# Two more matrix products as block pairs of seven products, with the gates computed first

## Chip, core and metric

The kernel runs on one core of one Trainium2 chip. The metric is the time of one execution in microseconds of the device. TensorE (PE, with its weight loads PEld) multiplies, VectorE (DVE) and ScalarE (ACT) do the elementwise work, GpSimd (POOL) does next to nothing, and SyncE (SP) issues nearly all the transfers.

## The reference

A trunk of two layers on 512 tokens of width 1024, everything in float32. What matters here, for each layer:

```python
h = rmsnorm(x, g_mix)
z = h @ w_in          # q, k, v | ret q, k, v, g | gate_a | gate_b
A = sliding_window_sink_attention(...)          # 512 x 512
r = retention(...) * rsqrt(mean(r * r)) * silu(rg)   # 512 x 1024
mixed = sigmoid(gate_a) * (A @ w_a) + sigmoid(gate_b) * (r @ w_b)
x = x + mixed @ w_out
h2 = rmsnorm(x, g_mlp)
x = x + square(relu(h2 @ w_up)) @ w_down        # width 4096
```

`w_b` and `w_out` are 1024 x 1024. After the second layer comes a final rmsnorm.

## The kernel before

**Layout.** All activations lie transposed: 128 features on the partitions, 512 tokens along the free dimension, eight such tiles for a width of 1024. Each float32 operand is split into `hi` (rounded for the fast matmul format) and `lo` (the rest), and a product is three matmuls, hi x hi, hi x lo and lo x hi (lines 280 to 282, in `products`). ScalarE makes `hi` by a copy and VectorE `lo` by a subtraction, for activations in `split` and for weights in `split_until` (lines 235 and 236).

**Weights.** They come in units of 128 x 1024, in an order written out in `unit_order`. When a unit is taken (`unit`), the units up to three further on are split, and the loads run three ahead of the splits. There are three buffers each for raw units, `hi` and `lo`. So the fourth unit on can be split only when TensorE has finished this one.

**Products.** `chunk` makes one output tile from one unit (24 matmuls of 512 columns), `group` four output tiles from four units, with four PSUM banks at a time. `pair` makes two output tiles of the up product as a block product: the inputs are halved along the features and the tokens halved as well (`H` = 256), and seven products of such blocks, with sums and differences of blocks as operands, replace eight. Its weights come as four parts. `load_part` loads two units, and `add_part` forms the sums of the weights on VectorE (lines 207 to 215). The sums of the moving operand are made once a layer by `sum_input`, called from hooks inside the first up group, and split into `sums`. The seven products gather in three banks `a`, `e` and `b`; ScalarE copies `a` to `b` midway (line 1037), and VectorE finishes the two tiles.

**Order in a layer.** First come attention and retention, partly in the background between products. Then four `gate_b` tiles (lines 911 to 925), the rest of retention (`drain`), a group of four `w_b` tiles, the other four `gate_b` tiles by `chunk`, and four `w_b` tiles by `chunk`. `put_mixed` (lines 930 to 938) multiplies each `w_b` tile with its gate, adds the gated attention part, which stands in `x`'s buffer, and splits the sum into slots of its own. Then `x` is loaded again, four `w_out` tiles are made by a group and four by chunks, and `put_x` (lines 956 to 961) adds each to `x`, makes the scaled and split input `xh`, `xl` of the up product from it, and adds its square to the sum for the norm. The `w_up` group follows, and `rstd` of the norm is finished in its hooks (`first_hooks`). After it come two up pairs, and then down products and up pairs in turn (`mlp_sequence`). Tile's planner orders the instructions of each engine by a timeline of its own.

Of the kernel before, what the change touches and what calls it, by code (L numbers as in the profile page):

```python
# [17 lines left out]
P = 128  # L18
# [30 lines left out]
DELAY = 2  # L49


def unit_order():

    order = [("w_in", i) for i in range(4 + 2 + 8 + 2 + 4 + 2)]
    order += [("w_in", i) for i in range(22, 26)]
    order += [("w_a", i) for i in range(4)]
    order += [("w_in", i) for i in range(26, 42)]
    order += [("w_b", i) for i in range(4)]
    order += [("w_in", i) for i in range(42, 46)]
    order += [("w_b", i) for i in range(4, 8)]  # L60
    order += [("w_out", i) for i in range(8)]
    for what, q, i in mlp_sequence():
        if what == "first":
            order += [("w_up", u) for u in range(4)]
        elif what == "pair":
            order += [("pair", 8 * q + 2 * i, part) for part in range(4)]
# [48 lines left out]
def decoder(ctx, tc, xT, x_first, w_in, w_a, w_b, w_out, w_up, w_down, tables, decay, band, out):  # L115
# [17 lines left out]
    def big(name, dtype=F32):  # L133
        return tmp.tile([P, 2, T], dtype, tag="big", name=name, bufs=6)
# [57 lines left out]
    def load_part(i):  # L192
        layer, _, j, part = order[i]
        if part == 0:
            raws[i] = raw_tile()
            nc.sync.dma_start(raws[i][:, LEFT], w_up[layer, j][:, LEFT])
            raws[i + 3] = raw_tile()
            nc.sync.dma_start(raws[i + 3], w_up[layer, j + 1])
        elif part == 1:
            raws[i] = big("raw2").rearrange("p a t -> p (a t)")  # L200
            nc.sync.dma_start(raws[i][:, RIGHT], w_up[layer, j][:, RIGHT])

    def add_part(i):
        part = order[i][3]
# [12 lines left out]
    def split_until(n):  # L217
        while state["split"] < min(n, len(order)):
# [12 lines left out]
            for at in (LEFT,) if paired and order[i][3] == 3 else halves(i):  # L231
# [94 lines left out]
    def group(name, layer, moving, evacuates, meanwhile=None):  # L326
# [3 lines left out]
        for u in range(4):  # L330
            hi, lo = unit(name, layer)
            for j in range(2):
                k = 2 * u + j
                for c, ps in enumerate(banks):
                    cols = slice(j * T + c * P, j * T + (c + 1) * P)
                    products(ps, [((hi[:, cols], lo[:, cols]), moving[k])], k == 0, k == KD - 1)
# [5 lines left out]
    def two_chunks(name, layer, moving, evacuates):  # L342
# [9 lines left out]
        for ps, evacuate in zip(banks, evacuates):  # L352
            evacuate(ps)

# [125 lines left out]
    def layer_body(layer):  # L480
# [276 lines left out]
        rg, rg_next = {}, {}  # L757

        def put_rg(i):
            def put(ps):  # L760
                if i % 2 == 0:
                    two = big("z")
# [14 lines left out]
        ret = {}  # L777
# [7 lines left out]
        class Head:  # L785
# [53 lines left out]
            def finish(self):  # L839
                h = self.h  # L840
                for e in range(2):
# [5 lines left out]
                    ret[2 * h + e] = (hi, lo)  # L847
# [69 lines left out]
        def gate_tile(c):  # L917
            if c % 2 == 0:
                two = big("gb")
                gates.extend(two[:, j, :] for j in range(2))  # L920
# [9 lines left out]
        def put_mixed(c):  # L930
            def put(ps):
                m = temp("m")
                nc.vector.tensor_tensor(m, ps, gates[c], ALU.mult)
                nc.vector.tensor_tensor(m, m, mixed[c], ALU.add)
                hi, lo = slots.one(), slots.one()
                split(view(hi), view(lo), m)
                ms[c] = (hi, lo)

            return put

        rT = [tuple(view(s) for s in ret[k]) for k in range(KD)]
        group("w_b", layer, rT, [put_mixed(c) for c in range(4)])
        for c in range(4, KD):
            gate_tile(c)
            chunk("w_in", layer, xs, gate(gates[c]))
        for c in range(4, KD):
            chunk("w_b", layer, rT, put_mixed(c))
        for k in range(KD):
            slots.give(*ret.pop(k))
# [13 lines left out]

        mT = [tuple(view(s) for s in ms[k]) for k in range(KD)]
        group("w_out", layer, mT, [put_x(c) for c in range(4)])
        for c in range(4, KD):
            chunk("w_out", layer, mT, put_x(c))
        for k in range(KD):
            slots.give(*ms.pop(k))
# [5 lines left out]
        H = T // 2  # L975
        sums = [slots.four() for _ in range(4)]
        by_form = [t[0].rearrange("p a (b t) -> p (a b) t", t=H) for t in sums]

        def sum_input(ks):
# [6 lines left out]
            (b11, b12), (b21, b22) = ((t[:, :, :H], t[:, :, H:]) for t in b)  # L986
            f = [big("sums").rearrange("p a (b t) -> p (a b) t", t=H) for _ in range(2)]
            t1, t2, t3, t4 = f[0][:, 0:2, :], f[0][:, 2:4, :], f[1][:, 0:2, :], f[1][:, 2:4, :]
            hi, lo = by_form[ks // 2], by_form[2 + ks // 2]
            nc.vector.tensor_tensor(t1, b12, b11, ALU.subtract)  # L990
            nc.vector.tensor_tensor(t2, b22, t1, ALU.subtract)
            split(hi[:, 0:4, :], lo[:, 0:4, :], f[0])
            nc.vector.tensor_tensor(t3, b22, b12, ALU.subtract)
            nc.vector.tensor_tensor(t4, b21, t2, ALU.subtract)
            split(hi[:, 4:8, :], lo[:, 4:8, :], f[1])

        def form(j):
            return [tuple(by_form[2 * i + k // 2][:, 2 * j + k % 2, :] for i in range(2)) for k in range(4)]

        def block(half, tokens):  # L1000
            at = slice(tokens * H, tokens * H + H)
            return [(xh[:, k, at], xl[:, k, at]) for k in range(4 * half, 4 * half + 4)]
# [20 lines left out]
        def pair(q):  # L1023
            def multiply(ps, weights, left, moving, start=True):
                hi, lo = weights
                cols = [slice((0 if left else 4 * P) + k * P, (0 if left else 4 * P) + (k + 1) * P) for k in range(4)]
                products(ps, [((hi[:, c], lo[:, c]), m) for c, m in zip(cols, moving)], start, True, not start)

            a, e, b = (bank(ps_mm, "mm")[:, :H] for _ in range(3))
            eu, z = temp("eu"), big("z")
            part = unit("pair", layer)
            multiply(a, part, True, block(0, 0))
            nc.scalar.activation(b, a, AF.Copy)  # L1037
            multiply(e, part, False, form(0))
            nc.scalar.activation(eu[:, :H], e, AF.Copy)
            part = unit("pair", layer)  # L1040
            multiply(b, part, True, form(1), False)
            nc.scalar.activation(eu[:, H:], b, AF.Copy)
            multiply(a, part, False, block(1, 0), False)
            nc.vector.scalar_tensor_tensor(z[:, 0, :H], a, 0.0, rms_mlp.value[:, :H], ALU.max, ALU.mult)  # L1044
            part = unit("pair", layer)
            multiply(b, part, True, form(2), False)
            nc.vector.tensor_tensor(z[:, 1, H:], b, eu[:, :H], ALU.add)
            multiply(e, part, False, block(1, 1), False)
            nc.vector.tensor_tensor(z[:, 0, H:], e, eu[:, H:], ALU.add)
            part = unit("pair", layer)  # L1050
            multiply(b, part, True, form(3), False)
            later = rms_mlp.value[:, H:].unsqueeze(1).broadcast_to([P, 2, H])
            nc.vector.scalar_tensor_tensor(z[:, :, H:], z[:, :, H:], 0.0, later, ALU.max, ALU.mult)
            nc.vector.scalar_tensor_tensor(z[:, 1, :H], b, 0.0, rms_mlp.value[:, :H], ALU.max, ALU.mult)
            hi, lo, own = up_home()
            for i in range(2):
                nc.scalar.activation(z[:, i, :], z[:, i, :], AF.Square)
                split(hi[:, i, :], lo[:, i, :], z[:, i, :])
                up[q].append((hi[:, i, :], lo[:, i, :]))
            up_slots[q].extend(own)  # L1060
# [18 lines left out]
        for what, q, i in mlp_sequence():  # L1079
            if what == "first":  # L1080
                group("w_up", layer, xs, [put_up] * 4, first_hooks())
            elif what == "pair":
                pair(q)
                if (q, i) == (3, 3):
                    for t in sums:
                        slots.give(*t[1])
# [79 lines left out]

def _up_units(w):

    units = _units_group(w, np.arange(T))
    for i, u in enumerate(_units_chunks(w, np.arange(T, D_FF))):  # L1170
        units.append(np.concatenate([u[:, UNIT // 2 :], u[:, : UNIT // 2]], 1) if i % 2 else u)
    return units
# [41 lines left out]
def _laid_out(x, g_mix, w_in, sinks, w_a, w_b, w_out, g_mlp, w_up, w_down, g_final):  # L1214
# [13 lines left out]
        "w_b": _stack(w_b, _half_grouped),  # L1228
        "w_out": _stack(w_out, _half_grouped),
# [24 lines left out]
```

## Time and profile before

| | |
|---|---|
| median of 3 runs | 1512.94 us (1510.96 to 1513.03) |
| profiled execution, first to last instruction | 1511.4 us |
| granted TensorE clock, mean | 0.998 |
| transfers | 155.10 MB, mean 103 GB/s |

The profiled execution has no other time than its span; the median of the runs is 1.5 us above it. A busy PE in the page is modelled from overlapping matmuls, so the cost of one is read from the steps between starts. Idle time of an engine counts only where TensorE waits for it.

### The profile page before, as it was taken

How to read it: one execution, taken by the hardware profiler on the slowest of the kernel's cores; microseconds unless marked ns; L12 is line 12 of the kernel's file. 1: busy time of each engine (PE TensorE's matmuls, PEld its weight loads, DVE VectorE, ACT ScalarE, POOL GpSimd, SP SyncE). 2: the span in 40 equal slices, each digit the busy share in tenths (PEclk: the TensorE clock that was granted, in tenths of full speed). 3: DMA queues.
4: the chain of work that ended last, by engine and by line, in shares of the span. 5: the costliest groups of instructions: out<-in, count | busy, mean ns of one | idle time of the engine just before them, and what ended most of it. 6: DMA issues, size and time to landing. Idle time of an engine off the chain costs nothing.

```text
span 1511.4 us, 20498 instructions
## 1 busy us (share of the span) xinstructions
PE 1499.2 (99%) x8080; PEld 1302.2 (86%) x8080; DVE 1026.7 (68%) x1598; ACT 740.1 (49%) x1163; POOL 2.9 (0%) x13
## 2 busy tenths in 40 slices
PE   9999999999999999999999999999999999999997
PEld 7888888888888999989888888888888999889997
DVE  6877668754787666676678765777449866666664
ACT  6656455632564444444455742555327544444452
POOL 0000000000000000000000000000000000000000
PEclk9999999999999999999999999999999999999999
DMA  6422322233223232233442222222342232232331
GB/s 217 123 97 75 98 79 91 70 125 126 98 78 104 98 112 97 93 104 115 165 131 93 84 84 98 82 79 84 126 125 98 85 104 92 99 111 98 103 108 56
DMA packets 52640, 155.10 MB, mean 103 GB/s; under 512 B 6208, under 2 KB 8384, under 8 KB 52544
## 3 DMA queue, kind: packets, MB, share of 16 engines
q1 hardware_dynamic: 52400, 153.54, 30.6%
q8 instruction: 63, 1.03, 0.3%
q14 instruction: 33, 0.27, 0.1%
q10 hardware_dynamic: 144, 0.26, 0.0%
HBM read 146.96 MB, written 4.19 MB: 100 GB/s over the span
## 4 chain that ended last, share of the span: by engine, by line
PE 98%; ACT 1%; DVE 0%; DMA 0%; issue 0%; DVEq 0%
PE mm L280 29%; PE mm L281 29%; PE mm L282 29%; PE rv L280 2%; PE rv L281 2%; PE rv L282 2%; PE score L651 1%; PE pT L616 1%; PE r L281 1%; PE r L282 1%; PE r L280 1%; PE pv L637 0%; PE pv L636 0%; PE ssq L374 0%; PE ret L281 0%; PE ret L282 0%
## 5 line engine op out<-in xcount | busy, mean ns | idle before, releaser
L235 ACT ACTIVATE hi<-raw 128x1024 fp32r<-128x1024 f32 (+1 forms) x313 | 314.6, 1013 | 517.9 <-PE mm L281 430.6
L236 DVE TENSOR_TENSOR lo<-raw,hi 128x1024 fp32r<-128x1024 f32 (+1 forms) x314 | 362.6, 1164 | 162.0 <-ACT hi L235 161.1
L281 PE MATMUL mm<-r,hi 128*128 128x512 f32 (+1 forms) x1136 | 392.5, 346 | 0.0
L280 PE MATMUL mm<-r,hi 128*128 128x512 f32 (+1 forms) x1136 | 389.5, 346 | 1.0 <-ACT mm L1037 1.0
L282 PE MATMUL mm<-r,lo 128*128 128x512 f32 (+1 forms) x1136 | 388.5, 346 | 0.0
L280 PE MATMUL mm<-xh,hi 128*128 128x512 f32 (+1 forms) x1008 | 358.2, 357 | 0.9 <-ACT xh L290 0.9
L281 PE MATMUL mm<-xl,hi 128*128 128x512 f32 (+1 forms) x1008 | 356.8, 356 | 0.0
L282 PE MATMUL mm<-xh,lo 128*128 128x512 f32 (+1 forms) x1008 | 355.4, 356 | 0.0
L280 PEld LDWEIGHTS mm<-r,hi 128*128 128x128 f32 x1136 | 214.8, 189 | 27.8 <-ACT mm L1037 1.4
L281 PEld LDWEIGHTS mm<-r,hi 128*128 128x128 f32 x1136 | 215.3, 189 | 26.3
L282 PEld LDWEIGHTS mm<-r,lo 128*128 128x128 f32 x1136 | 215.0, 189 | 25.7
L280 PEld LDWEIGHTS mm<-xh,hi 128*128 128x128 f32 x1008 | 191.1, 190 | 27.1 <-ACT xh L290 1.6
L281 PEld LDWEIGHTS mm<-xl,hi 128*128 128x128 f32 x1008 | 191.3, 190 | 25.5
L282 PEld LDWEIGHTS mm<-xh,lo 128*128 128x128 f32 x1008 | 191.0, 190 | 25.5
L1064 DVE TENSOR_TENSOR x<-x,mm 128x512 f32<-128x512 f32 x56 | 37.8, 687 | 34.2 <-PE mm L282 34.2
L282 PE MATMUL rv<-hi,xl 128*128 128x512 f32 x128 | 49.8, 389 | 0.0
L281 PE MATMUL rv<-lo,xh 128*128 128x512 f32 x128 | 49.8, 389 | 0.0
L280 PE MATMUL rv<-hi,xh 128*128 128x512 f32 x128 | 49.4, 391 | 0.0
L281 PE MATMUL mm<-ulo,hi 128*128 128x512 f32 (+1 forms) x128 | 46.3, 363 | 0.0
L280 PE MATMUL mm<-uhi,hi 128*128 128x512 f32 (+1 forms) x128 | 46.2, 362 | 0.0
L282 PE MATMUL mm<-uhi,lo 128*128 128x512 f32 (+1 forms) x128 | 45.7, 365 | 0.0
L1044 DVE SCALAR_TENSOR_TENSOR z<-mm,rstd 128x256 f32<-128x256 f32 x28 | 11.9, 425 | 42.0 <-PE mm L282 42.0
(188 smaller groups left out, 1682.1 us busy)
## 6 DMA issues: line engine op xcount, KB each, us to landing
raw<-w_in_in SPq DMA_DIRECT2D x89, 512.0 KB, 3.3
raw<-w_down_in SPq DMA_DIRECT2D x64, 512.0 KB, 3.3
raw<-w_up_in SPq DMA_DIRECT2D x36, 512.0 KB, 3.3
raw<-w_up_in SPq DMA_DIRECT2D x56, 256.0 KB, 2.7
raw<-w_b_in SPq DMA_DIRECT2D x16, 512.0 KB, 3.2
raw<-w_out_in SPq DMA_DIRECT2D x16, 512.0 KB, 3.5
raw<-w_a_in SPq DMA_DIRECT2D x8, 512.0 KB, 3.3
x<-xT_in SPq DMA_DIRECT2D x15, 256.0 KB, 3.6
```

Source lines behind the costliest of these rows:

```text
L235: nc.scalar.activation(hi[:, at], raw[:, at], AF.Copy)
L236: nc.vector.tensor_tensor(lo[:, at], raw[:, at], f32(hi[:, at]), ALU.subtract)
L280: nc.tensor.matmul(ps, ah, bh, start=start and i == 0, stop=False, **more)
L281: nc.tensor.matmul(ps, ah, bl, start=False, stop=False, **more)
L282: nc.tensor.matmul(ps, al, bh, start=False, stop=stop and i == n - 1, **more)
L616: nc.tensor.transpose(pt[:, i * P : (i + 1) * P], sm[:, at : at + P], ident)
L651: nc.tensor.matmul(ps[:, g * w : (g + 1) * w], q_s[g][:, c, at], part[:, keys], start=i == 0, stop=i == 1)
L1044: nc.vector.scalar_tensor_tensor(z[:, 0, :H], a, 0.0, rms_mlp.value[:, :H], ALU.max, ALU.mult)
L1064: nc.vector.tensor_tensor(x[:, c, :], x[:, c, :], ps, ALU.add)
```

## The change

- `pair` becomes a function of the layer, the tiles of the moving operand, the forms and a `Sink` that finishes the two tiles; the up product uses it through `Up`. The forms move into a class `Forms`, which takes its slots as they are added.
- `w_b` is made by four pairs, in the order of tiles 0, 4, 2, 6 (`B_PAIRS`). The forms of `ret` are added during the late gates, from the tiles `zs` in which the retention output stands.
- All eight `gate_b` tiles are made ahead of `w_b`.
- `Mixed` finishes a `w_b` pair: two gate products per token half on VectorE, one add of the gated attention part on GpSimd for both tiles, and a split into `xh` and `xl`, in which the normalised input stood until then.
- `w_out` makes four tiles by a group, which takes the tiles in the order `OUT_TILES` (0, 1, 4, 5, 2, 3, 6, 7), and four by two pairs. The forms of the mixed values are added in hooks of that group. `Out` adds the pairs to `x`.
- As `xh` and `xl` hold the mixed values during `w_out`, the scaled input of the up product is made within the last `w_out` pair.
- The shared pool of two-tile buffers has nine instead of six, with a smaller scratch for descriptors.
- On the host, `w_b` and half of `w_out` are laid out for pairs.

```diff
+B_PAIRS = (0, 4, 2, 6)
+OUT_TILES = (0, 1, 4, 5, 2, 3, 6, 7)
...
-    order += [("w_in", i) for i in range(26, 42)]
-    order += [("w_b", i) for i in range(4)]
-    order += [("w_in", i) for i in range(42, 46)]
-    order += [("w_b", i) for i in range(4, 8)]
-    order += [("w_out", i) for i in range(8)]
+    order += [("w_in", i) for i in range(26, 46)]
+    order += [("pair", "w_b", c, part) for c in B_PAIRS for part in range(4)]
+    order += [("w_out", i) for i in range(4)]
+    order += [("pair", "w_out", c, part) for c in (4, 6) for part in range(4)]
...
-        return tmp.tile([P, 2, T], dtype, tag="big", name=name, bufs=6)
+        return tmp.tile([P, 2, T], dtype, tag="big", name=name, bufs=9)
...
+    class Forms:
...
+        def add(self, ks, b):
+
+            (b11, b12), (b21, b22) = ((t[:, :, :H], t[:, :, H:]) for t in b)
+            f = [big("sums").rearrange("p a (b t) -> p (a b) t", t=H) for _ in range(2)]
+            t1, t2, t3, t4 = f[0][:, 0:2, :], f[0][:, 2:4, :], f[1][:, 0:2, :], f[1][:, 2:4, :]
+            nc.vector.tensor_tensor(t1, b12, b11, ALU.subtract)
+            nc.vector.tensor_tensor(t2, b22, t1, ALU.subtract)
+            self.keep(ks, 0, f[0])
+            nc.vector.tensor_tensor(t3, b22, b12, ALU.subtract)
+            nc.vector.tensor_tensor(t4, b21, t2, ALU.subtract)
+            self.keep(ks, 2, f[1])
+
+        def keep(self, ks, first, f):
+            t, own = slots.four()
...
+            split(hi, lo, f)
...
+    def pair(layer, tiles, form, sink):
...
+        a, e, b = (bank(ps_mm, "mm")[:, :H] for _ in range(3))
+        eu = temp("eu")
+        part = unit("pair", layer)
+        multiply(a, part, True, block(tiles, 0, 0))
+        nc.scalar.activation(b, a, AF.Copy)
+        multiply(e, part, False, form[0])
+        nc.scalar.activation(eu[:, H:], e, AF.Copy)
+        part = unit("pair", layer)
+        multiply(b, part, True, form[1], False)
+        nc.scalar.activation(eu[:, :H], b, AF.Copy)
+        multiply(a, part, False, block(tiles, 1, 0), False)
+        sink.one(a)
+        sink.two(eu)
+        part = unit("pair", layer)
+        multiply(b, part, True, form[2], False)
+        sink.three(b, eu[:, H:])
+        multiply(e, part, False, block(tiles, 1, 1), False)
+        sink.four(e, eu[:, :H])
+        part = unit("pair", layer)
+        multiply(b, part, True, form[3], False)
+        sink.done(b)
...
         for c in range(4):
-            gate_tile(c)
-            chunk("w_in", layer, xs, gate(gates[c]))
+            gated(c)
         drain()
-
+        ret_sums = Forms()
+        for c in range(4, KD):
+            if c < 6:
+                ret_sums.add(2 * c - 8, (zs.pop(c - 4), zs.pop(c - 2)))
+            gated(c)
...
+        class Mixed(Sink):
...
+            def one(self, a):
+                nc.vector.tensor_tensor(self.m[:, 0, :H], a, self.gate[:, 0, :H], ALU.mult)
+
+            def three(self, b, eu):
+                nc.vector.tensor_tensor(self.m[:, 1, H:], b, eu, ALU.add)
+
+            def four(self, e, eu):
+                nc.vector.tensor_tensor(self.m[:, 0, H:], e, eu, ALU.add)
+
+            def done(self, b):
+                m, two = self.m, slice(self.c, self.c + 2)
+                nc.vector.tensor_tensor(m[:, 1, :H], b, self.gate[:, 1, :H], ALU.mult)
+                nc.vector.tensor_tensor(m[:, :, H:], m[:, :, H:], self.gate[:, :, H:], ALU.mult)
+                nc.gpsimd.tensor_tensor(m, m, x[:, two, :], ALU.add)
+                split(xh[:, two, :], xl[:, two, :], m)
+                ms[self.c] = m
...
+        for c in B_PAIRS:
+            pair(layer, rT, ret_sums, Mixed(c))
+        slots.give(*ret_slots)
+        ret_sums.free()
...
+        m_sums = Forms()
...
                 nc.vector.tensor_tensor(x[:, c, :], x[:, c, :], ps, ALU.add)
-                scaled_input(c, g_mlp)
                 squared_input(c, g_mlp)
...
+        class Out(Sink):
...
+            def two(self, eu):
+                xa = x[:, self.c : self.c + 2, H:]
+                nc.vector.tensor_tensor(xa, xa, eu.rearrange("p (a t) -> p a t", t=H), ALU.add)
+                if self.c == 6:
+                    for k in range(4):
+                        scaled_input(k, g_mlp)
...
+            def four(self, e, eu):
+                self.add(0, slice(H, T), e)
+                if self.c == 6:
+                    for k in (4, 5):
+                        scaled_input(k, g_mlp)
+
+            def done(self, b):
+                self.add(1, slice(0, H), b)
+                for k in (self.c, self.c + 1):
+                    if k > 5:
+                        scaled_input(k, g_mlp)
+                    squared_input(k, g_mlp)
+
+        group(
+            "w_out",
+            layer,
+            xs,
+            [put_x(c) for c in range(4)],
+            {0: lambda: m_sums.add(0, (ms[0], ms[4])), 1: lambda: m_sums.add(2, (ms[2], ms[6]))},
+            OUT_TILES,
+        )
+        for c in (4, 6):
+            pair(layer, xs, m_sums, Out(c))
+        m_sums.free()
...
-    nc = bacc.Bacc("TRN2", target_bir_lowering=False, num_devices=1)
+    nc = bacc.Bacc("TRN2", target_bir_lowering=False, num_devices=1, dynamic_dma_scratch_size=1024)
```

More of the change, by code (lines that the diff above doesn't have):

```diff
@@ L65, in unit_order @@
         elif what == "pair":
-            order += [("pair", 8 * q + 2 * i, part) for part in range(4)]
+            order += [("pair", "w_up", 8 * q + 2 * i, part) for part in range(4)]
         elif what == "down":
@@ L324, in chunk, with group @@
         evacuate(ps)
-    def group(name, layer, moving, evacuates, meanwhile=None):
+    def group(name, layer, moving, evacuates, meanwhile=None, tiles=range(KD)):
         banks = [bank(ps_mm, "mm") for _ in range(4)]
@@ L353, in two_chunks, with __init__, __getitem__, free @@
             evacuate(ps)
+    H = T // 2
+    class Forms:
+        def __init__(self):
+            self.parts, self.slots = {}, []
+        def add(self, ks, b):
[10 more added lines that the diff above has]
+            t, own = slots.four()
+            self.slots.extend(own)
+            hi, lo = (t[:, 2 * i : 2 * i + 2, :].rearrange("p a (b t) -> p (a b) t", t=H) for i in range(2))
+            split(hi, lo, f)
+            for j in range(2):
+                for i in range(2):
+                    self.parts[first + j, ks + i] = (hi[:, 2 * j + i, :], lo[:, 2 * j + i, :])
+        def __getitem__(self, j):
+            return [self.parts[j, k] for k in range(4)]
+        def free(self):
+            slots.give(*self.slots)
@@ new lines, in block, with multiply @@
+    def block(tiles, half, tokens):
+        at = slice(tokens * H, tokens * H + H)
+        return [(hi[:, at], lo[:, at]) for hi, lo in tiles[4 * half : 4 * half + 4]]
+    class Sink:
+        def one(self, a):
+            pass
+        def two(self, eu):
+            pass
+        def three(self, b, eu):
+            pass
+        def four(self, e, eu):
+            pass
+        def done(self, b):
+            pass
+    def pair(layer, tiles, form, sink):
+        def multiply(ps, weights, left, moving, start=True):
+            hi, lo = weights
+            cols = [slice((0 if left else 4 * P) + k * P, (0 if left else 4 * P) + (k + 1) * P) for k in range(4)]
+            products(ps, [((hi[:, c], lo[:, c]), m) for c, m in zip(cols, moving)], start, True, not start)
+        a, e, b = (bank(ps_mm, "mm")[:, :H] for _ in range(3))
[19 more added lines that the diff above has]
+        sink.done(b)
@@ L915, in layer_body, with gated @@
         gates = []
-        def gate_tile(c):
+        def gated(c):
             if c % 2 == 0:
-                two = big("gb")
-                gates.extend(two[:, j, :] for j in range(2))
+                gates.append(big("gb"))
+            chunk("w_in", layer, xs, gate(gates[c // 2][:, c % 2, :]))
         for c in range(4):
-            gate_tile(c)
-            chunk("w_in", layer, xs, gate(gates[c]))
+            gated(c)
         drain()
-        ms = {}
[L930 to L949, printed above, removed]
+        ret_sums = Forms()
[3 more added lines that the diff above has]
+            gated(c)
@@ L958, in put, with __init__, add, one @@
                 nc.vector.tensor_tensor(x[:, c, :], x[:, c, :], ps, ALU.add)
-                scaled_input(c, g_mlp)
                 squared_input(c, g_mlp)
             return put
[L964 to L977, printed above, removed]
+        class Out(Sink):
+            def __init__(self, c):
+                self.c = c
+            def add(self, i, at, ps):
+                xa = x[:, self.c + i, at]
+                nc.vector.tensor_tensor(xa, xa, ps, ALU.add)
+            def one(self, a):
+                self.add(0, slice(0, H), a)
+            def two(self, eu):
+                xa = x[:, self.c : self.c + 2, H:]
[3 more added lines that the diff above has]
+                        scaled_input(k, g_mlp)
+            def three(self, b, eu):
+                self.add(1, slice(H, T), b)
+            def four(self, e, eu):
+                self.add(0, slice(H, T), e)
+                if self.c == 6:
+                    for k in (4, 5):
+                        scaled_input(k, g_mlp)
+            def done(self, b):
+                self.add(1, slice(0, H), b)
[14 more added lines that the diff above has]
+        m_sums.free()
+        sums = Forms()
         def sum_input(ks):
@@ L985, in sum_input @@
                     nc.scalar.activation(b[part][:, i, :], x[:, g, :], AF.Copy, scale=gain[:, col : col + 1])
[L986 to L1002, printed above, removed]
+            sums.add(ks, b)
         up = [[] for _ in range(4)]
@@ L1021, in up_home @@
             return big("uhi", F32R), big("ulo", F32R), []
[L1023 to L1060, printed above, removed]
@@ L1082, in layer_body @@
             elif what == "pair":
-                pair(q)
+                pair(layer, xs, sums, Up(q))
                 if (q, i) == (3, 3):
-                    for t in sums:
-                        slots.give(*t[1])
+                    sums.free()
             elif what == "down":
```

70 lines of the change are left out of this document (52 added, 18 removed).

## The prediction

> **What bounds the kernel now.** I read the page first, then the waits of TensorE, then single instructions of the timeline, and last a table of stretches of layer 0.
>
> ```profile
> span 1511.4 us, 20498 instructions
> PE 1499.2 (99%) x8080; PEld 1302.2 (86%) x8080; DVE 1026.7 (68%) x1598; ACT 740.1 (49%) x1163; POOL 2.9 (0%) x13
> ...
> PE mm L280 <- ACT mm L1037: 1.0, 2, 0.5
> ...
> 303.20:325.00 21.80, 21.80 (x98) 18.06 (x97) 8.64 (x10) 6.27 (x8) 0.00 (x0) 1.00 0.31 101
> 325.00:368.50 43.50, 43.50 (x193) 36.03 (x193) 25.36 (x33) 14.82 (x19) 0.00 (x0) 1.00 0.41 136
> 368.50:390.30 21.80, 21.80 (x98) 18.06 (x97) 6.80 (x7) 4.88 (x5) 0.00 (x0) 1.00 0.36 115
> 390.30:433.90 43.60, 43.60 (x194) 36.09 (x194) 41.06 (x51) 29.19 (x39) 0.00 (x0) 1.00 0.29 95
> 433.90:454.10 20.20, 19.68 (x155) 19.09 (x154) 16.59 (x25) 14.62 (x25) 0.00 (x0) 1.00 0.22 78
> 454.10:475.00 20.90, 20.90 (x133) 18.96 (x133) 13.80 (x20) 9.27 (x13) 0.00 (x0) 1.00 0.30 102
> 303.20:454.10 150.90, 150.38 (x732) 127.33 (x731) 98.44 (x126) 69.77 (x96) 0.00 (x0) 1.00 0.33 108
> ```
>
> The second line is the page's: TensorE (PE) is busy for 1499.2 of 1511.4 us. The wait row says that inside the layers it waits 1.0 us in all, twice 0.5 us, at the first pair after the first-quarter up group. So the time is the sum of TensorE's steps, and nothing is won by closing gaps. The stretches (columns: length, then busy time of PE, PEld, DVE, ACT, POOL, clock, DMA) follow the code of layer 0. To 325.0 runs the `w_b` group, to 368.5 the four late gates and the four `w_b` chunks, to 390.3 the `w_out` group, to 433.9 the four `w_out` chunks and the `w_up` group, to 454.1 the first two up pairs. VectorE (DVE) is at rest for over half of the first three (40.8 of 87.1 us busy), but busy for 41.06 of 43.60 us in the fourth: the stretch before the up pairs is already full.
>
> What one matmul costs is its step from start to start, since the durations overlap.
>
> ```profile
> 232.98 0.39 PE L280 MATMUL rv<-hi,xh 128*128 128x512 f32 x1
> ...
> 240.91 0.39 PE L282 MATMUL rv<-hi,xl 128*128 128x512 f32 x1
> ...
> 444.09 0.28 PE L280 MATMUL mm<-r,hi 128*128 128x256 f32 x1
> ...
> 448.99 0.28 PE L282 MATMUL mm<-r,lo 128*128 128x256 f32 x1
> ...
> L280 PEld LDWEIGHTS mm<-r,hi 128*128 128x128 f32 x1136 | 214.8, 189 | 27.8 <-ACT mm L1037 1.4
> ```
>
> Between the first two rows lie 35 steps of 512 columns: 7.93/35 = 0.2266 us. Between the next two lie 41 steps of 256 columns: 4.90/41 = 0.1195 us. That is 0.53 of the wide one, not 0.50; the weight load of 189 ns that each matmul brings is the same for both.
>
> **TensorE's share.** Two output tiles by chunk or group are 2 x 8 x 3 = 48 wide matmuls, 48 x 0.2266 = 10.88 us. A pair is 7 products x 4 x 3 = 84 narrow ones, 84 x 0.1195 = 10.04 us. One pair saves 0.84 us; an eighth of the work would be 1.36. There are four pairs for `w_b` and two for `w_out` in each layer, so 6 x 0.84 = 5.0 us a layer, 10.1 us in all. TensorE will show 2 x 6 x 36 = 432 more instructions, 8512.
>
> **VectorE's share.** The pairs are paid in VectorE's time. The steps of its instructions, back to back:
>
> ```profile
> 406.56 0.68 DVE L991 TENSOR_TENSOR sums<-xg,sums 128x512 f32<-128x512 f32 x1
> 407.16 0.69 DVE L993 TENSOR_TENSOR sums<-xg 128x512 f32<-128x512 f32 x1
> ...
> 409.28 1.22 DVE L288 TENSOR_TENSOR r<-sums,r 128x1024 fp32r<-128x1024 f32 x1
> 410.41 0.69 DVE L990 TENSOR_TENSOR sums<-xg 128x512 f32<-128x512 f32 x1
> ...
> 445.52 0.42 DVE L1049 TENSOR_TENSOR z<-mm,eu 128x256 f32<-128x256 f32 x1
> 445.86 0.41 DVE L1047 TENSOR_TENSOR z<-mm,eu 128x256 f32<-128x256 f32 x1
> ```
>
> A step is 0.60 us for 512 elements, 1.13 for 1024, 0.34 for 256 out of PSUM. From these, for one layer:
> - The forms of the moving operand, `Forms.add`, twice for `ret` and twice for the mixed values: 8 x 0.60 + 4 x 1.13 = 9.3 us a set, 18.6 us for both.
> - The weights of a pair: four sums of 512, three `lo` of 1024 and one of 512, 4 x 0.60 + 3 x 1.13 + 0.60 = 6.4 us, where two plain units took 2 x 1.13 = 2.3. That is +4.1 us, six times: 24.8 us.
> - Evacuation in `Mixed`: 4 x 0.34 + 0.60 + 1.13 = 3.1 us for two tiles instead of 6 x 0.60 = 3.6, as the add of the attention half goes to GpSimd: -2.0 us for four pairs.
> - Evacuation in `Out`: 4 x 0.34 + 0.60 = 2.0 us instead of 1.2: +1.5 us for two pairs.
>
> The sum is +42.9 us. The last row of the table then reads 98.44 + 42.9 = 141.3 us of VectorE in 150.9 - 5.0 = 145.9 us of TensorE: 97%. So what matters is where this work falls. Stage by stage, work against TensorE's time:
> - Gates 4 to 7 (21.8 us). Of the 8.64 us of the first row four `lo` are 4.5; the other 4.1 are left over from the retention heads. With four gate products 2.4, the `ret` forms 9.3, and the weights 1.1 + 5.8 (three units are prepared ahead): 22.7 us, 0.9 over.
> - Four `w_b` pairs (40.2 us): 0.6 + 3 x 6.4 for pair weights, 3.4 for the first `w_out` units, 12.4 - 2.1 for evacuation: 33.5 us.
> - `w_out` group (21.8 us): 2.1 + 9.3 for forms + 1.1 + 5.8 = 18.3 us.
> - Two `w_out` pairs and the `w_up` group (20.1 + 21.8 = 41.9 us): the 41.06 us of the fourth row, plus 5.9 for the second pair's weights in place of a plain unit, plus 1.5: 48.5 us. This is 6.6 us more than TensorE takes.
> - First two up pairs: unchanged, 16.59 of 20.2 us, 3.6 free; then 20.9 - 13.80 = 7.1 free.
>
> So the backlog of 6.6 us meets 3.6 us of free time behind it. What may be late is the second half of the up forms, the third weight part and the `up` values; what may not is `rstd` and the first weight parts, without which TensorE stands at the first up pair. The stall lies between 0 (the two free stretches take it all) and 6.6 us (nothing can be put off); I take 6.6 - 3.6 = 3.0 us a layer.
>
> **Waits and moves.** A pair that follows a group waits for its third bank, copied by ScalarE: 0.5 us at the up stage now (the row of L1037). The first `w_out` pair stands at such a place too: between 0 and 0.5 us, I take 0.5. The other pairs follow pairs, and the second up pair has no such wait: 0.
>
> The gates moved ahead bring their four unit loads with them. On SP's queue these pass the `w_b` loads, and nothing is added to the sum of bytes that a layer needs: 0, since the unit loads below land in 3.2 us and three units, over 7 us even of narrow parts, are loaded and split ahead. The reload of `x`, 16 transfers in both layers, is issued once GpSimd's add has read `x`; the weights behind it on SP can wait up to one add. That is covered by the 5.4 us that each `w_out` unit lasts (24 x 0.2266).
>
> GpSimd's add itself has no row here. The nearest is a fill of the same size:
>
> ```profile
> L514 POOL MEMSET r<- 128x1024 f32 x2 | 1.9, 955 | 696.4 <-PE mm L281 696.4
> raw<-w_b_in SPq DMA_DIRECT2D x16, 512.0 KB, 3.2
> ```
>
> One write of 1024 elements takes 0.96 us; with two reads counted like the write an add is at most 2.9 us. By the latter it still ends long before the `w_out` group needs the values of its pair, except for the last (tiles 6 and 7), which that group reads in its fourth unit, 16 us later. ScalarE's split `xh` waits for it, and the copy of the bank for the next pair and the next `hi` queue behind that split. The 12 narrow matmuls of the second product, 1.4 us, cover a part: between 0 and 2.9 - 1.4 = 1.5 us a pair. I take 0, as the split can be ordered behind those copies.
>
> [...] ScalarE does not become a bound: it has 69.77 us of 150.9 now, and even half of what VectorE gets would leave it at 91 of 145.9.
>
> **The sum.** Against the profiled execution, whose span is 1511.4: -10.1 + 2 x (3.0 + 0.5) = -3.1, so 1508.3 us. The median of the runs shown, 1512.94, is 1.5 above that span; at that distance the time is 1509.8 us, 0.21% below before. A measurement of this kernel can tell about 0.2% (3.0 us) from no change.
>
> **The rivals.**
> - The cover holds. VectorE's backlog is put off into the up pairs and the 7.1 us behind them, and only the 0.5 us remains: -10.1 + 1.0, so 1503.8 us. For it: in the fourth row VectorE is at 94% and TensorE loses nothing; the order of each queue is planned. Against: that was 94%, not 116%.
> - VectorE becomes the bound at the `w_up` group: nothing of the 6.6 us can be put off, since `rstd` needs the squares of the last tiles, which now end with the second `w_out` pair. Then 2 x 7.1 - 10.1 = +4.1, so 1517.0 us, slower. It decides from a stall of 5.0 us a layer on, the gain of six pairs. For it: those two stretches are the fullest; the first up pair already waits. Against: half of the up forms is not needed until the third and fourth part of that pair.
> - GpSimd's add holds VectorE, whose instructions nearly all read two tensors from SBUF, while it runs. At 2.9 us the `w_b` pairs come to 0.9 + 33.5 + 3 x 2.9 = 43.1 us against 40.2 and the group to 18.3 + 2.9 = 21.2 against 21.8, so 2.9 us more a layer: 1515.6 us. At 0.96 us it is 37.3 and costs nothing.
>
> [...]
>
> **How the numbers follow.** The forecast has 0.40 (own range 1506 to 1514; 0.18 of it below 1509.9, 0.02 above 1516.0), the cover that holds 0.22, the bound at the `w_up` group 0.20, GpSimd's hold 0.18 (of the last two 0.06 within 0.2%). That makes 0.40 faster, 0.26 the same, 0.34 slower. The range runs from the first rival's 1503.5 to 1521, short of the 1522.8 that both slow rivals give together; about 2 in 10 lie outside.
>
> **What would show it.** 8512 TensorE instructions at unchanged steps, 0.23 and 0.12 us. Six more stretches of 10.0 us a layer where two tiles took 10.9. VectorE near 97% from the late gates to the second up pair, with TensorE's idle time, some 3 us a layer, at the first up pair, released by VectorE or by `rstd`. Idle time of TensorE within the `w_b` pairs, with VectorE's instructions stretched while POOL is busy, would mean GpSimd's hold. A narrow step over 0.13 us with `w_b` would make the first term wrong; waits on DMA inside pairs would make the cover of the loads wrong.

## The result, and the profile after

The change makes the kernel slower: 1531.41 us (median of 4 runs, 1529.92 to 1532.69) against 1512.18 us for the kernel before, a ratio of 1.0126 with a 95% interval of 1.0111 to 1.0140. The profiled execution spans 1530.5 us, 19.1 us more than before, where the prediction had 3.1 us less, and its range ended at 1521.

The head of the page of the changed kernel, its waits of TensorE, and stretches of it as for the kernel before (length, then PE, PEld, DVE, ACT, POOL, the granted TensorE clock, DMA):

```profile
span 1530.5 us, 21626 instructions
PE 1497.5 (98%) x8512; PEld 1318.5 (86%) x8512; DVE 1120.8 (73%) x1730; ACT 784.9 (51%) x1231; POOL 25.1 (2%) x21
...
PE mm L284 <- DVE lo L238: 13.0, 10, 2.0
PE mm L282 <- DVE up L1138: 7.8, 2, 4.0
PE mm L282 <- ACT eu L434: 0.8, 2, 0.4
PE mm L282 <- DVE x L1065: 0.7, 2, 0.3
...
303.20:463.20 160.00, 149.12 (x946) 135.27 (x945) 145.26 (x191) 92.04 (x129) 11.06 (x4) 0.99 0.32 102
...
446.00:449.00 3.00, 3.00 (x17) 3.00 (x18) 2.88 (x5) 3.00 (x7) 0.00 (x0) 0.57 0.02 5
```

TensorE, which waited 1.0 us inside the layers before, now waits 13.0 us for the `lo` of weights and 7.8 us for VectorE's evacuation of the `w_up` group. Both come in nearly equal parts from the two layers (6.4 and 6.6 us, 3.8 and 4.0 us), at the same places. In layer 0 the waits stand here (timeline of TensorE, rows with idle time before them):

```profile
343.79 0.39 PE L284 MATMUL mm<-r,lo 128*128 128x256 f32 x1 [0.91 <-DVE lo L238]
348.53 0.38 PE L284 MATMUL mm<-r,lo 128*128 128x256 f32 x1 [1.60 <-DVE lo L238]
357.66 0.39 PE L284 MATMUL mm<-r,lo 128*128 128x256 f32 x1 [1.68 <-DVE lo L238]
362.39 0.38 PE L284 MATMUL mm<-r,lo 128*128 128x256 f32 x1 [1.60 <-DVE lo L238]
374.46 0.96 PE L284 MATMUL mm<-xh,lo 128*128 128x512 f32 x3 [0.58 <-DVE lo L238]
398.42 0.39 PE L282 MATMUL mm<-r,hi 128*128 128x256 f32 x1 [0.35 <-DVE x L1065]
413.93 0.39 PE L282 MATMUL mm<-r,hi 128*128 128x256 f32 x1 [0.38 <-ACT eu L434]
...
441.77 0.28 PE L284 MATMUL mm<-xh,lo 128*128 128x256 f32 x1
445.85 0.39 PE L282 MATMUL mm<-r,hi 128*128 128x256 f32 x1 [3.80 <-DVE up L1138]
...
446.83 0.41 PE L282 MATMUL mm<-r,hi 128*128 128x256 f32 x1
...
448.96 0.41 PE L283 MATMUL mm<-r,hi 128*128 128x256 f32 x1
```

The first four are in the second and third `w_b` pair, the fifth at the start of the `w_out` group, and the last wait is in the first up pair. An idle figure understates the loss: the step from 441.77 to 445.85 is 4.08 us for an idle time of 3.80, where an undisturbed step is 0.12, and the step that follows a wait is 0.22 (343.79 to 344.01). So each wait costs about 0.26 us more than it shows. After the long one the clock is granted at 0.57, and ten steps take 2.13 us, 0.213 each instead of 0.12, for some 16 matmuls: 1.5 us. The layer's sum: 10.9 us of idle time in eight waits, 2.1 for their steps, 1.5 for the clock, less the 0.8 us that before lost at its one wait, is 13.7. Less the 5.0 us that the pairs save that is 8.7 us; the first down product's evacuation comes 9.1 us later than before (478.3 against 469.2).

What goes on in the first of these waits is seen on VectorE and GpSimd (timelines of the two engines):

```profile
339.71 0.68 DVE L212 TENSOR_TENSOR raw<-raw 128x512 f32<-128x512 f32 x1
340.31 4.03 DVE L238 TENSOR_TENSOR lo<-raw,hi 128x1024 fp32r<-128x1024 f32 x2
344.26 0.41 DVE L1033 TENSOR_TENSOR m<-mm,gb 128x256 f32<-128x256 f32 x1
...
340.04 2.61 POOL L1045 TENSOR_TENSOR m<-m,x 128x1024 f32<-128x1024 f32 x1 [337.40 <-DVE m L1043]
```

GpSimd's add runs from 340.04 to 342.65. VectorE's row of 4.03 us joins two `lo`, one of 1024 elements and one of 512. Singly, the first takes 3.42 us, from 340.31 to 343.73, and the second 0.68. A `lo` of 1024 elements takes 1.22 us elsewhere; this one ends 1.1 us after GpSimd has. That is 2.2 us lost to VectorE, just ahead of the weights that TensorE waits for. The next two adds of this layer cost VectorE 2.2 and 1.8 us in the same way. The fourth, from 382.79 to 386.13, meets VectorE mostly idle and costs it 0.2 us. Together that is 6.4 us in layer 0.

Ahead of the next held `lo` (again two in one row, the first of 3.41 us), VectorE waits for weights. Here are two loads of a pair's second unit as SyncE issues them, and VectorE's rows behind the second:

```profile
335.40 0.33 SPq L200 DMA_DIRECT2D raw<-w_b_in  x1
348.50 0.33 SPq L200 DMA_DIRECT2D raw<-w_b_in  x1
...
347.27 1.21 DVE L238 TENSOR_TENSOR lo<-raw,hi 128x1024 fp32r<-128x1024 f32 x1
...
352.65 0.69 DVE L209 TENSOR_TENSOR raw<-raw 128x512 f32<-128x512 f32 x1 [2.11 <-DMA raw<-w_b_in]
...
354.20 4.01 DVE L238 TENSOR_TENSOR lo<-raw,hi 128x1024 fp32r<-128x1024 f32 x2
```

The load at 348.50 is issued as the `lo` from 347.27 ends, which frees a raw buffer, and VectorE stands idle for 2.11 us until it has landed.

### The profile page after: what moved, and what is told of

It reads as the page before. It is cut to its first block, busy times and chain, and to the rows that moved or that the text cites. A ratio compares the mean times of both kernels' runs of the same rounds, so it can differ in the third digit from the quotient of the medians.

```text
span 1530.5 us, 21626 instructions
## 1 busy us (share of the span) xinstructions
PE 1497.5 (98%) x8512; PEld 1318.5 (86%) x8512; DVE 1120.8 (73%) x1730; ACT 784.9 (51%) x1231; POOL 25.1 (2%) x21
## 4 chain that ended last, share of the span: by engine, by line
PE 88%; DVE 7%; issue 2%; DMA 2%; ACT 1%; DVEq 0%; ACTq 0%
PE mm L282 25%; PE mm L283 25%; PE mm L284 25%; DVE lo L238 2%; PE rv L282 2%; PE rv L284 2%; PE rv L283 2%; PE score L743 1%; PE pT L708 1%; DMA raw<-w_b_in 1%; PE r L283 1%; PE r L284 1%; PE r L282 1%; ACT hi L237 0%; DVE xl L290 0%
## 5 line engine op out<-in xcount | busy, mean ns | idle before, releaser
L238 DVE TENSOR_TENSOR lo<-raw,hi 128x1024 fp32r<-128x1024 f32 (+1 forms) x338 | 396.4, 1183 | 115.8 <-ACT hi L237 114.9
L282 PE MATMUL mm<-xh,hi 128*128 128x512 f32 (+1 forms) x1120 | 395.5, 356 | 0.7 <-ACT xh L292 0.7
L283 PE MATMUL mm<-xl,hi 128*128 128x512 f32 (+1 forms) x1120 | 395.1, 355 | 0.0
L284 PE MATMUL mm<-xh,lo 128*128 128x512 f32 (+1 forms) x1120 | 389.7, 355 | 1.2 <-DVE lo L238 1.2
L284 PE MATMUL mm<-r,lo 128*128 128x256 f32 (+1 forms) x1168 | 372.2, 323 | 11.8 <-DVE lo L238 11.8
L282 PE MATMUL mm<-r,hi 128*128 128x256 f32 (+1 forms) x1168 | 373.5, 323 | 9.2 <-DVE up L1138 7.8
L283 PE MATMUL mm<-r,hi 128*128 128x256 f32 (+1 forms) x1168 | 375.6, 322 | 0.0
L284 PEld LDWEIGHTS mm<-xh,lo 128*128 128x128 f32 x1120 | 211.7, 189 | 30.3 <-DVE lo L238 2.6
L282 PEld LDWEIGHTS mm<-xh,hi 128*128 128x128 f32 x1120 | 212.3, 190 | 29.4 <-ACT xh L292 1.4
L283 PEld LDWEIGHTS mm<-xl,hi 128*128 128x128 f32 x1120 | 212.4, 190 | 27.8
L209 DVE TENSOR_TENSOR raw<-raw 128x512 f32<-128x512 f32 x40 | 27.8, 696 | 26.2 <-DMA raw<-w_up_in 12.8
```

The costliest lines, as they stand in the source:

```text
L209: nc.vector.tensor_tensor(raws[i][:, RIGHT], w2[:, RIGHT], w2[:, LEFT], ALU.add)
L282: nc.tensor.matmul(ps, ah, bh, start=start and i == 0, stop=False, **more)
L283: nc.tensor.matmul(ps, ah, bl, start=False, stop=False, **more)
L284: nc.tensor.matmul(ps, al, bh, start=False, stop=stop and i == n - 1, **more)
```

## The experiments

Theory H: GpSimd's add holds VectorE while it reads. Theory B: VectorE's backlog makes the wait at the first up pair. The rivals are named with each run.

**The add on VectorE, and no add at all.**

```diff
-                nc.gpsimd.tensor_tensor(m, m, x[:, two, :], ALU.add)
+                nc.vector.tensor_tensor(m, m, x[:, two, :], ALU.add)
```

> The changed kernel with one instruction moved: the add of the attention half in Mixed runs on VectorE instead of GpSimd. Theory H (while GpSimd's add reads SBUF, VectorE's next instruction stands): the changed kernel loses 6.4 us of TensorE idle time a layer inside the four w_b pairs and the start of the w_out group, 7.7 us with the slower first steps behind each wait; VectorE now has 1.1 us more per pair but is never held, so nearly all of that goes: 1531 - 2 x (7.7 - 1.5) = about 1519 us, and no lo of 1024 elements shows a duration above 1.3 us. Rival W (the pair weights alone are too much for VectorE, GpSimd is innocent): 4 x 1.1 us more work a layer, so 1531 to 1540 us and the waits within the pairs stay. Both leave the 4 us wait at the first up pair.

1520.22 us (span 1517.9), a ratio to before of 1.0063 (1.0048 to 1.0078). In each layer one wait is left in the `w_b` pairs, of 1.20 and of 1.71 us, and no `lo` takes longer than 1.23 us. VectorE has the four adds of a layer to do as well, and the kernel is 11 us faster than with them on GpSimd.

> The changed kernel without the add of the attention half (the mixed values are the gated retention part alone), so neither GpSimd nor VectorE does it. Theory H: the waits inside the w_b pairs go, 2 x 7.7 us less, about 1516 us. Rival W: the waits inside the pairs stay at over 1 us each and the time stays within 4 us of 1531.

The same line left out. 1517.52 us (span 1515.3); no wait for `lo` at all. The add on VectorE costs 2.6 us of span against none; on GpSimd it costs 15.2. Rival W falls: the pair weights alone leave no wait.

**What of GpSimd holds VectorE.** Both runs start from the kernel with the add on VectorE and add GpSimd work that nobody waits for, after the last read of the gate tile.

```diff
+                for _ in range(3):
+                    nc.gpsimd.memset(self.gate, 0.0)
```

> The kernel with the add on VectorE (profiled span 1517.9 us), and behind it GpSimd fills the gate tile, which nobody reads any more, three times (3 x 0.96 = 2.9 us a pair): as long as the add was, but it only writes. Theory H (it is the reading of SBUF by GpSimd that holds VectorE): the span stays within 2 us of 1518 and VectorE's lo of 1024 elements stays at 1.2 us. Rival (any work of GpSimd in these pairs slows VectorE): 1528 us or more, with lo instructions of 2.5 us and longer.

1520.69 us, span 1517.1: the same as without.

```diff
+                nc.gpsimd.tensor_tensor(self.gate, self.gate, self.gate, ALU.add)
```

> The same kernel, with the add on VectorE, and behind it GpSimd adds the gate tile to itself: one add of 128 x 1024 per pair whose result nobody reads. Theory H: VectorE is held for about 1.8 us or more in each pair, on top of its own add, so TensorE waits in the pairs again: 1518 + 2 x 4 x 1.7 = about 1531 us, 1527 to 1537. Rival S (in the changed kernel the loss came from ScalarE's split, which waited for the add's result with other copies queued behind it): nobody waits for this add, so 1518 us within 2.

1534.43 us, span 1533.9, 16.0 us more than without it, for an add whose result nobody reads. Part of that is a slower clock: granted at 0.990 on the mean against 0.995, with steps of 0.21 us for 256 columns within the `w_b` pairs of both layers (among them from 359.69 to 362.68 us and from 1119.61 to 1120.46). The longest wait for `lo` is 3.3 us. The two timelines at the same place, first with the fills, then with the dead add:

```profile
338.16 1.22 DVE L238 TENSOR_TENSOR lo<-raw,hi 128x1024 fp32r<-128x1024 f32 x1
339.29 1.22 DVE L1045 TENSOR_TENSOR m<-m,x 128x1024 f32<-128x1024 f32 x1
...
337.85 2.99 POOL L1047 MEMSET gb<- 128x1024 f32 x3 [335.23 <-DVE m L1043]
```

```profile
338.61 2.92 DVE L238 TENSOR_TENSOR lo<-raw,hi 128x1024 fp32r<-128x1024 f32 x1
341.44 1.21 DVE L1045 TENSOR_TENSOR m<-m,x 128x1024 f32<-128x1024 f32 x1
...
338.33 2.10 POOL L1046 TENSOR_TENSOR gb<-gb 128x1024 f32<-128x1024 f32 x1 [335.69 <-DVE m L1043]
```

Beside 2.99 us of writing the `lo` takes its usual 1.22 us. Beside 2.10 us of reading it takes 2.92, that is, it ends at 341.53, 1.1 us after the add (338.33 + 2.10 = 340.43), as if it had started only then. Theory H is shown for this add, which reads SBUF; beside the fills, which only write, the `lo` of 1024 elements kept their mean of 1.22 us. Rival S, that the harm came from ScalarE's wait for the result, is not needed for it. ScalarE does wait for the add in the changed kernel, 12.6 us in six waits, and no run says whether any of that reaches TensorE.

**Each half of the change alone.** Both runs have the add on VectorE.

> The w_b half of the change alone, with the add on VectorE: w_out is made by a group and four chunks from the mixed values in xh and xl, and the scaled input of the up product is made behind the last chunk. Theory B (VectorE's backlog from the w_out pairs makes the 4 us wait at the first up pair, with the slow TensorE clock behind it): both go, 5.5 us, and the 1.2 us of waits at the w_out pairs as well, for 1.7 us a layer of TensorE steps more: against the kernel with the add on VectorE 2 x (6.7 - 1.7) = 10 us less, about 1509 us, a little below the kernel before. Rival R (the wait comes from making the scaled input and the squares late, behind the last w_out tile, whatever the weights cost): the wait at the first up pair stays at 3 us or more and the time is above 1515 us.

```diff
-    order += [("w_out", i) for i in range(4)]
-    order += [("pair", "w_out", c, part) for c in (4, 6) for part in range(4)]
+    order += [("w_out", i) for i in range(8)]
...
+        for c in range(4, KD):
+            chunk("w_out", layer, xs, put_x(c))
```

1510.72 us (span 1507.7), a ratio of 0.9998 (0.9988 to 1.0007): no difference to before that can be told, where 1509 was expected. There is no wait for banks at the first up pair, but 4.9 us for `lo` in six places. Rival R, by which the late scaled input and squares would keep that wait at 3 us or more, does not fit this.

> The w_out half of the change alone: w_b is made by a group and four chunks as before, with all gates first and the mixed values, added on VectorE, in xh and xl; half of w_out by two pairs as changed. Theory B: the waits at the w_out pairs and the first up pair stay (6.7 us a layer with the slow clock) and the pairs save 1.7 us a layer: 1511.4 + 2 x (6.7 - 1.7) = about 1522 us, with no wait in the w_b stretch. Rival (the backlog at the up group comes down from the w_b pairs): the first up pair waits under 1 us and the time is at 1508 to 1512 us.

```diff
-    order += [("pair", "w_b", c, part) for c in B_PAIRS for part in range(4)]
+    order += [("w_b", i) for i in range(8)]
...
+        group("w_b", layer, rT, [put_mixed(c) for c in range(4)])
+        for c in range(4, KD):
+            chunk("w_b", layer, rT, put_mixed(c))
```

1522.56 us (span 1520.9), a ratio of 1.0071 (1.0054 to 1.0088). Two `w_out` pairs a layer, without any `w_b` pair, bring the wait at the first up pair back, 3.12 us in each layer instead of 3.80 and more, with steps of 0.21 us behind it in layer 0 (mean granted clock 0.995). So that wait belongs to the `w_out` half, as theory B has it. This run alone does not exclude rival R, since the scaled input is late here as well; the next run is for that.

**What makes the wait at the first up pair.** From the kernel with the add on VectorE, the third and fourth form of the up product are left out:

```diff
...
             self.keep(ks, 0, f[0])
+            if part:
+                for j in range(2):
+                    for i in range(2):
+                        self.parts[2 + j, ks + i] = self.parts[j, ks + i]
+                return
...
-            sums.add(ks, b)
+            sums.add(ks, b, True)
```

> The kernel with the add on VectorE, and the second half of the up product's forms left out (the third and fourth form stand for the first and second, so the up pairs are computed from the wrong sums): 4 x 0.60 + 2 x 1.13 = 4.7 us less of VectorE ahead of the first up pair, while the chain of squares, rstd and its reciprocal stays. Theory B (backlog of VectorE): the wait of 3.8 to 4.7 us at the first up pair falls under 1 us, the slow clock behind it goes, 1518 - 2 x 4.5 = about 1509 us. Rival R (the chain to rstd is too long in itself): the wait stays above 3 us and the span above 1515.

1515.08 us (span 1513.4), not 1509. The wait falls from 3.80 us to 1.00 in layer 0, and from 4.75 to 1.0 in layer 1, and the steps behind it are back at 0.12 us in layer 0 (mean granted clock 0.998 against 0.995). So the work left out, VectorE's and two copies by ScalarE, makes most of it, and the chain to `rstd` is not too long in itself. But the other waits grow, from 2.9 to 5.8 us for `lo` and from 0.8 to 2.3 us at the `w_out` pairs, so half of the gain is lost elsewhere.

**Other banks.** The first up pair waits because its second and third bank are still to be emptied by `put_up`, which needs `rstd`. Three banks of another pool stand idle at that time. The run starts from the kernel with the add on VectorE.

```diff
-        a, e, b = (bank(ps_mm, "mm")[:, :H] for _ in range(3))
+        a, e, b = (bank(p, n)[:, :H] for p, n in ((ps_mm, "mm"), (ps_aux, "pe"), (ps_aux, "pb")))
```

> The kernel with the add on VectorE, and two of the three banks of a pair (e and b) taken from the three banks that serve attention and the norms and stand idle here. The first up pair then needs no bank of the up group before, so it does not wait for rstd. If the wait there was only one for banks, it goes with the slow clock behind it, and the 0.4 us at the w_out pair as well: 1518 - 2 x (5.5 + 0.5) = about 1506 us, below the kernel before. If VectorE's backlog reaches the weights of the first two up pairs as well, TensorE waits for their lo instead, 2 to 4 us a layer: 1510 to 1516 us.

1508.62 us (span 1506.2), a ratio of 0.9978 (0.9969 to 0.9988): faster than the kernel before. VectorE has as much to do as with the add on VectorE alone (busy for 1115.4 us, against 1117.2); from the late gates into the first up pair it is busy for 139 of 146 us. The waits of TensorE now (the waits of this kernel, then of its timeline the stretch mentioned):

```profile
PE mm L284 <- DVE lo L238: 5.2, 5, 1.5
PE warm L262 <- DVE ones L257: 1.1, 1, 1.1
PE mm L282 <- ACT xh L292: 0.6, 1, 0.6
PE ssq L531 <- ACT sq L523: 0.5, 1, 0.5
...
300.00:446.00 146.00, 143.61 (x918) 130.57 (x917) 139.04 (x189) 88.21 (x123) 0.00 (x0) 1.00 0.32 111
```

TensorE waits for `put_up` no more: in layer 0 it begins the second product of the first up pair at 432.80, and `put_up` begins at 435.88. The backlog is worked off behind that point.

> The kernel before with only the banks e and b of its up pairs taken from the idle three. It waited 0.5 us twice for a bank, so 1510.5 us, the same as before within the noise. If it were faster by more than 2 us, the gain of the pairs with their own banks would not be the pairs'.

1511.19 us, a ratio of 1.0000 (0.9990 to 1.0009). The banks alone give the kernel before nothing.

> The w_b half of the change with the add on VectorE and these banks, w_out by group and chunks. It had no wait for banks, only 4.9 us for lo, so the banks give it nothing: 1507 to 1508 us of span. Against all six pairs with banks (1506.2 us) the two w_out pairs are then worth 1 to 2 us in both layers together, less than the 3.4 us of TensorE's steps that they save.

1510.60 us (span 1507.8), a ratio of 0.9994 (0.9984 to 1.0004), as expected: without `w_out` pairs there is no wait for banks. All six pairs span 1.6 us less. By the medians it is 2.0 us; the two intervals overlap, so the worth of the `w_out` pairs is not settled.

> The change as it stands, add on GpSimd, with the banks e and b of the pairs from the idle three. Theory: the two losses are separate, GpSimd's hold in the w_b pairs (7 us a layer) and the wait for banks at the first up pair with the slow clock (5.5 us a layer). The second goes, the first stays: 1530.5 - 2 x 5.5 = about 1519 us. If the hold only delays what is then late at the first up pair, the time falls below 1512 us.

The changed kernel, add on GpSimd, with these banks: 1522.67 us (span 1521.0). The banks save 9.5 us of span where 11 were expected; 14.3 us of waits for `lo` remain. So the two losses are mostly separate ones.

## Why the prediction was wrong

**TensorE's term was right.** 8512 instructions, as said, and narrow steps at 0.12 us. With the two losses removed, the span is 1506.2 us, 5.2 below before, against the 10.1 us that the steps save; 5.2 us of waits for `lo` are most of the difference.

**VectorE's load was right as well.** The prediction had 141.3 us from the late gates to the second up pair; the stretch from 303.2 to 463.2 has 145.26, and the 6.4 us of holds by GpSimd are in it. It was nearly full, as said, but not the bound by sum.

**GpSimd's add was the step that failed first.** That the add holds VectorE was set aside as a rival with a chance of 0.18, and the forecast took 0 for it. The rival itself had the hold right and the size wrong: 2.9 us a layer. It took each of a layer's four holds as 2.9 us, where they were 2.2, 2.2, 1.8 and 0.2 us in layer 0, and it let them use up VectorE's free time in the `w_b` stretch first (40.2 against 33.5 us). The measured loss was 12.6 us of span in both layers, 6.3 a layer (1530.5 against 1517.9), and 7.6 against no add at all.

That free time could not take up the holds, by what the traces show. It was in part idle time ahead of loads, which the prediction counted as covered, at 0. VectorE waits for the loads of `w_b` in six places, 9.5 us in all. A load of a pair's second unit needs a raw buffer, which a `lo` frees, and the sums for the next pair need that load. So VectorE's work, a hold and a load stand in one loop. From the load at 335.40 to the one at 348.50 it takes 13.1 us, against 10.4 us (335.05 to 345.44) in the run without the add, and TensorE needs 10.0 us for a pair. A hold therefore lengthens a loop that had no room left. Without the add VectorE still waits 5.6 us for these loads, and TensorE waits for no `lo`. No run takes the loads out of the loop, so their part is read from the traces and not shown by an experiment. The sign that the prediction names, waits on DMA inside pairs, is there, at VectorE.

The traces show the hold from both sides. In layer 0 of the changed kernel a `lo` of 1024 elements that VectorE takes up while the add runs ends 1.08 or 1.09 us after it (343.73 against 342.65, 357.61 against 356.52, 369.39 against 368.30), and a `lo` beside fills took its usual 1.22 us. For the add itself the prediction had at most 2.9 us, an estimate from the 0.96 us of a fill. The chip took 2.40 to 3.34 us, 2.78 on average. The 2.40 us are those of an add that began while VectorE stood idle (365.90, and the same in layer 1). Of the longest in layer 0, 1.1 us lie beside a `lo` that VectorE had started just before (382.65 to 383.87), so VectorE held GpSimd as well.

**The stall at the first up pair was mis-sized, and its path was not seen.** The prediction took 3.0 us a layer, the backlog of 6.6 less the 3.6 free behind it. The run showed 3.8 to 4.0 us of idle time and 5.5 us of loss. Its subtraction assumed that the backlog could be worked off behind the start of the first up pair, and it named the `up` values among what may be late. But the pair needed banks that only `put_up` frees, the function that makes these values. VectorE in layer 0 of the changed kernel, while TensorE stood from 441.89 to 445.85:

```profile
439.57 3.35 DVE L468 RECIPROCAL rstd<-rstd 128x512 f32<-128x512 f32 x1 [0.43 <-ACT rstd L467]
442.84 0.63 DVE L209 TENSOR_TENSOR raw<-raw 128x512 f32<-128x512 f32 x1
443.38 1.21 DVE L238 TENSOR_TENSOR lo<-raw,hi 128x1024 fp32r<-128x1024 f32 x1
444.51 2.48 DVE L1138 SCALAR_TENSOR_TENSOR up<-mm,rstd 128x512 f32<-128x512 f32 x4
```

For the first 1.0 us `rstd` was not ready, as the second rival had it. For the next 1.6 us a sum and a `lo` of weights stood ahead of `put_up`, and the first two of its four evacuations took the other 1.3 us. What made `rstd` late is open: TensorE takes up `sl`, the `lo` part of the squares, only at 438.42, though VectorE had it ready at 433.39, and no run separates that order from VectorE's backlog. Given other banks, the same backlog cost no wait there.

**The clock was not thought of.** A wait of 3.8 us cost 1.5 us more in steps of 0.213 us.

**The wait taken as 0.5 us at the first `w_out` pair** was 0.35 us, for VectorE; a second of 0.38 us, for a copy by ScalarE, came in the second pair, where 0 was taken. TensorE waited for no load.

**A slip in the range.** The prediction calls its lower end, 1503.5 us, the first rival's time; that rival's sum gives 1503.8.

## What to carry to other kernels

Where VectorE prepares operands just in time for TensorE, be wary of moving one of its adds to GpSimd. Here an add of 1024 elements that reads SBUF held VectorE's subtractions for up to 2.2 us, and VectorE needs 1.14 us to do that add itself (339.43 to 340.57 in `add_on_vector`). An engine's free time in a sum is not room for more work if it stands there waiting for a load. When work is added to a nearly full engine, look not only at the sum but at the instruction that frees something, a bank here, and at what stands ahead of it in the queue; here three idle banks brought 11.7 us of span, and 4.7 us a layer of work left out brought 4.5. A change that loses can hold a gain: both losses undone, this one beats the kernel before by 0.2%.

## What the runs showed of the hardware

- A VectorE `lo` of 1024 elements took 3.42 us instead of 1.22 beside a GpSimd add of 1024 elements in the changed kernel, and one took 2.92 beside an add with no data in common (`dead_add_on_gpsimd`). Beside three GpSimd fills it took 1.22 (`fill_on_gpsimd`).
- After 4.08 us from one matmul's start to the next the clock was granted at 0.57 over the next 3 us (changed kernel, layer 0), with steps of 0.213 us for 256 columns. Steps of 0.21 us also followed such gaps of 3.39 us (`w_out_pairs_only`, layer 0), of 5.03 us (`add_on_vector`, layer 1) and of 2.01 us (`dead_add_on_gpsimd`, layer 1, from 1154.99 on). After gaps of 1.28 us (`half_the_up_forms`, layer 0), 1.96 us (changed kernel, layer 0) and 2.02 us (`dead_add_on_gpsimd`, layer 0) the steps were back at 0.12 us from the second on. So the length of the gap alone does not tell the two apart, and no run shows what else does.
